# A hybrid encoder layer: the down projection as seven block products, and a first up tile evacuated product by product

## The chip, the cores and the metric

The kernel runs on one core of a Trainium2 chip. The metric is the device time of one execution in microseconds. Engines are named as in the profile: PE (TensorE), PEld (its weight loads), DVE (VectorE), ACT (ScalarE), POOL (GpSimd) and SP (SyncE, which issues nearly all transfers).

## The reference, cut to what matters

The layer is an attention mixer and a gated delta-rule mixer, then a feed-forward block with a causal convolution, then a per-layer embedding, and a last RMSNorm. Model width 1024, feed-forward width 2816, 1024 prompt frames and 8 x 16 sample frames, so T = 1152 columns. The change touches the feed-forward block alone:

```
h2 = _rmsnorm(x, norm_ffn)
u_gate, u_val = jnp.split(h2 @ w_up, [D_FF], axis=-1)
ext_f = jnp.concatenate([ffn_buf.astype(u_gate.dtype), u_gate], axis=1)
act = jax.nn.gelu(_causal_dwconv(ext_f, conv_ffn), approximate=True)
x = x + (act * u_val) @ w_down
gate_p = jax.nn.sigmoid(_rmsnorm(x, norm_ple) @ w_ple_gate)
x = x + gate_p * (p @ w_ple)
```

## The kernel before, in words

Everything is held transposed: features on the 128 partitions, frames along the columns. A float32 product is made of three fp32r matmuls: each operand is split into a rounded part H and a rest L, and the terms are wh x H, wh x L and wl x H. ACT makes H by a copy, DVE or POOL makes L by a subtraction.

**Who sets the order.** The program is recorded by coroutines. A driver (`_Driver`) keeps a planned clock for each engine and lets the thread go on that could start first; what it records is the fixed order of each engine's queue. `yield DVE` asks for an engine, `yield event` waits for another thread, `yield bank` takes a free buffer. `pick(DVE, POOL)` takes the engine whose planned clock is earlier.

**Up projection** (`up_products`, `evac_up`, `up_inner`). It has 22 tiles `ju[f]` of 128 + 128 features (gate and value). Each tile is seven half-size block products in the Strassen-Winograd manner, named A1X, S1T1, S2T2, A2X, S3T3, S4Y and B2T4; a product is 4 contraction tiles x 2 column halves x 3 terms = 24 matmuls of 288 columns. Three PSUM tiles `ups` serve them. The products in `CHAIN` are added onto an earlier product's PSUM tile, after that has been read (`kept`). The last read of a tile, of B2T4, multiplies by R2, the row factors of the RMSNorm. Sums of weight blocks (`up_sums`, tiles `s`) and weight splits (`up_rest`, tiles `wl`) are shared out by `pick`. `up_inner` does the convolution, the gelu and the product with the value half, and stores the 128 x 1152 result in DRAM as `AT[f]`.

**Down projection** (`jd`, `load_up`, `evac_down`). Three column blocks b of 384; in each two groups of four output row groups d; in each three pieces of the contraction (8, 8 and 6 tiles of 128). All weights are loaded and split again for every block, in three buffers (`down_weights`: wh/wl twice, T3H). The activations of a block are loaded from `AT` and split into the places that held the up projection's operands (B1, T0, T1, T2). `evac_down` multiplies by R2, adds the residual `x2T`, makes the operands H3/L3 of the gate and adds the squares to `ssq` (POOL).

**Gate blocks** (`gate`, `evac_pg`). Per block eight jobs of 24 matmuls of 384 columns on `w_ple_gate`; then a tanh, two multiply-adds on DVE and squares. The blocks 0 and 1 stand in the order after the first piece of the next column block's down products; block 2 is last. `final` scales and stores blocks 0 and 1, `last_rows` turns and stores block 2.

Two lines matter for the order of the row norms after the down projection: in `rms`, `if b < NB - 1: yield self.quarter[b + 1].done` holds block b's norm back until a job of the next block is through.

Of the kernel before, what the change touches and what calls it, by code (L numbers as in the profile page):

```python
# [297 lines left out]

def up_order(f):


    return (A1X, S1T1, A2X, S2T2, S4Y, S3T3, B2T4) if f == 0 else (A1X, S1T1, S2T2, A2X, S3T3, S4Y, B2T4)
# [6 lines left out]
class _Kernel:  # L309
# [95 lines left out]
    def down_loads(self):  # L405
# [6 lines left out]
        for j in self.jd:  # L412
# [35 lines left out]
    def down_weights(self, j, used):  # L448
# [14 lines left out]
        self.drv.spawn(self.down_rest(j, wh, wl), 1)  # L463
# [10 lines left out]
    def up_loads(self):  # L474

        nc = self.nc
        for j in self.ju:
# [8 lines left out]
            nc.sync.dma_start(g, self.I["w_up"][22 + j.f])  # L486
            nc.sync.dma_start(v, self.I["w_up"][j.f])
# [4 lines left out]
    def up_sums(self):  # L492
        nc, q = self.nc, {}
        for j in self.ju:
            yield j.loaded
            a1, a2, b1, b2 = j.raw
            for n in (0, 1, 3, 2) if j.f == 0 else range(4):
# [8 lines left out]
                e, w = self.pick(DVE, POOL) if j.f else (DVE, nc.vector)  # L506
                yield e
                (w.tensor_sub if n else w.tensor_add)(o, x, y)
# [3 lines left out]
    def up_weights(self, j, used):  # L512
# [8 lines left out]
        for i in up_order(j.f):  # L521
# [10 lines left out]
            self.drv.spawn(self.up_rest(j, i, wh, wl), 1 if j.f else 0)  # L532

    def up_rest(self, j, i, wh, wl):
        e, q = self.pick(DVE, POOL) if j.f else (DVE, self.nc.vector)
# [65 lines left out]
    def up_products(self, j):  # L601
        nc, drv = self.nc, self.drv
        bank = {}
        drv.spawn(self.evac_up(j, bank), 0 if j.f else -1)
        for i in up_order(j.f):
            yield j.prepared[i]
            wh, wl = j.w[i]
            if i in CHAIN:
                bank[i] = bank[CHAIN[i]]
                yield j.kept[CHAIN[i]]  # L610
            else:
                bank[i] = yield self.ups
            if (j.f, i) == (21, S3T3):
                drv.spawn(self.more_accs(), 1)
            first, own = i not in CHAIN, i in CHAIN
            for u in range(2):
                acc = bank[i][:, u, :288]
                for k in range(4):
# [4 lines left out]
                    nc.tensor.matmul(acc, wh[:, k], H, start=first and k == 0, stop=False, skip_group_check=own)  # L623
# [24 lines left out]
    def build(self):  # L648
# [28 lines left out]
        self.AT = dp.tile([22, 128, T], F32, name="AT")  # L677
        self.mixers()
        self.merge_ffn()

    def constants(self):
# [8 lines left out]
        t = cp.tile([128, 5], F32, name="ngd")  # L690
        self.ngd, self.ngf = t[:, 0:1], t[:, 1:5]
# [95 lines left out]
    def first_loads(self, jobs, p):  # L787
# [46 lines left out]
        nc.vector.tensor_scalar(self.ngf, self.nrm[:, 1, 0:4], -1.0, None, op0=OP.mult)  # L834
# [1596 lines left out]
    def merge_jobs(self):  # L2431
# [28 lines left out]
        self.aev = [[_Event() for _ in range(NB)] for _ in range(22)]  # L2460
        self.AB, self.H3, self.X4, self.jd, self.down = {}, {}, {}, [], []
        self.split3 = [_Event() for _ in range(4)]
        self.plev, self.aout = _Event(), [_Event() for _ in range(NB)]
        up = lambda k0: lambda k, cols: self.AB[k0 + k]

        self.piece, self.last = _Event(), None
# [3 lines left out]
        self.part_done, self.quarter = {}, {}  # L2470
# [7 lines left out]
        for b in range(NB):  # L2478
            for ds in (range(4), range(4, 8)):
                heads = {}  # L2480
                for k0, k1 in ((0, 8), (8, 16), (16, 22)):
                    if b and ds[0] == 0 and k0 == 8:

                        self.jd += gate(b - 1)
                    for d in ds:
                        j = _Job(I["w_down"][d][:, k0:k1], k1 - k0, up(k0), self.evac_down(d), blocks=(b,),
                                 pre=self.pre_down(d), late=True, head=heads.get(d), last=k1 == 22,
                                 need=lambda b, k, k0=k0: self.aev[k0 + k][b])
                        heads.setdefault(d, j)
                        self.jd.append(j)  # L2490
                        if k0 == 0 and d == 2:
                            self.quarter[b] = j
                        for f in range(k0, k1):
                            self.part_done[b, f] = j.done
        self.jd += gate(NB - 1)
        for j in self.ja+self.jo:
            j.merge = True
        a, b = self.jd[-8:-6]
        a.lag, a.twins, b.of = True, [b], a
        self.add_jobs(self.jpp + self.jb + self.ja + self.jo + self.ju + self.jd)  # L2500
# [121 lines left out]
    def evac_out(self, d):  # L2622
# [13 lines left out]
        def go(b, cols, acc, x):  # L2636
# [20 lines left out]
            if d < 4:  # L2657
# [5 lines left out]
                yield DVE  # L2663
                nc.vector.scalar_tensor_tensor(T1, lo, self.ngf[:, d:d + 1], T3, op0=OP.mult, op1=OP.add)
            else:
# [4 lines left out]
                yield from to(t, hi, T1, OP.subtract)  # L2670
# [29 lines left out]
    def up_parts(self, t):  # L2700
# [24 lines left out]
        if t == 3:  # L2725
            self.cs.views.append(self.hp.tile([128, 4, 2, 288], F32, name="T3")
                                 .rearrange("p a b c -> p (a b c)")[:, :T])
            self.cs.free.append((self.drv.cur.t, 0))

    def up_part(self, t, k, R, H, L, prev):  # L2730
# [4 lines left out]
        for b in range(NB):  # L2735
            self.drv.set(self.tev[t][k][b])

    def evac_up(self, j, bank):
# [8 lines left out]
        for i in up_order(f):  # L2747
# [3 lines left out]
            if i == S1T1 and f:  # L2751
                yield self.uev[f - 1]
            if i == B2T4:
# [7 lines left out]
                for e in self.Re[0]:  # L2761
                    yield e
                x = own(u3)
                q16 = lambda x: x.rearrange("p (b q) -> p b q", q=16)
                for o, i_, r in ((g[:, 1, :, :2], x[:, :, :2], R[:, 1, :, :2]),
                                 (ext[:, 962:1026], x[:, 0, 2, :64], self.R2[:, 960:TP]),
                                 (es[:, 0:2, 2:], q16(x[:, 0, 2, 64:]), q16(self.R2[:, TP:TP + 32])),
                                 (es[:, 2:8, 2:], q16(x[:, 1, 2]), q16(self.R2[:, TP + 32:]))):
                    yield DVE
                    nc.vector.tensor_mul(o, i_, r)  # L2770
# [551 lines left out]
```

## Time and profile before

| | |
|---|---|
| median of 3 runs | 2092.29 us (2091.4 to 2093.45) |
| the profiled execution | 2095.13 us, of which the span is 2093.4 us |
| granted clock, mean | 0.992 |
| PE busy | 2046.2 us, 98% of the span |
| DVE, ACT, POOL busy | 70%, 49%, 39% |
| up projection | 1190.9 to 1694.4 us |
| down projection and gate blocks | 1694.4 to 2082 us |
| last rows and output | 2082 to 2093.4 us |

A row of the windows view names a stretch in us from the span's start. `x` behind a busy time counts instructions. All work is recorded by helpers, so every line number is L192, and groups are told apart by their tiles: `up` and `dn` are the PSUM tiles of the two projections, `fe` the gate half with its convolution margin, `fv` the value half, `u` the partial sums of an up tile, `T` several tiles that take one another's place.

### The profile page before, as it was taken

How to read it: one execution, taken by the hardware profiler on the slowest of the kernel's cores; microseconds unless marked ns; L12 is line 12 of the kernel's file. 1: busy time of each engine (PE TensorE's matmuls, PEld its weight loads, DVE VectorE, ACT ScalarE, POOL GpSimd, SP SyncE). 2: the span in 40 equal slices, each digit the busy share in tenths (PEclk: the TensorE clock that was granted, in tenths of full speed). 3: DMA queues.
4: the chain of work that ended last, by engine and by line, in shares of the span. 5: the costliest groups of instructions: out<-in, count | busy, mean ns of one | idle time of the engine just before them, and what ended most of it. 6: DMA issues, size and time to landing. Idle time of an engine off the chain costs nothing.

```text
span 2093.4 us, 37189 instructions
## 1 busy us (share of the span) xinstructions
PE 2046.2 (98%) x13176; PEld 1997.7 (95%) x13176; DVE 1473.1 (70%) x3493; ACT 1034.4 (49%) x2057; POOL 816.3 (39%) x1025
## 2 busy tenths in 40 slices
PE   7999999999999999999999989999999999999998
PEld 6899999999999999989999989999999999999998
DVE  6268989998555687768465866666766675766656
ACT  5267667655634555676333433333333354535434
POOL 3344543532223534554363335555555500211102
PEclk9999999999999999999999999999999999999999
DMA  7343256776438564666664311212222266656542
GB/s 271 99 125 106 88 190 196 224 206 182 132 103 241 158 201 143 180 214 212 209 215 151 125 62 64 85 65 83 77 74 71 93 209 191 205 172 226 175 138 101
DMA packets 242697, 317.35 MB, mean 152 GB/s; under 512 B 40956, under 2 KB 200272, under 8 KB 242384
## 3 DMA queue, kind: packets, MB, share of 16 engines
q1 hardware_dynamic: 219712, 288.50, 44.6%
q10 hardware_dynamic: 22800, 26.49, 3.6%
q8 instruction: 104, 1.70, 0.3%
q14 instruction: 81, 0.66, 0.1%
HBM read 227.73 MB, written 88.81 MB: 151 GB/s over the span
## 4 chain that ended last, share of the span: by engine, by line
PE 53%; DVE 1%; DMA 1%; issue 0%; SPq 0%; ACT 0%; DVEq 0%; ACTq 0%
PE up L192 23%; PE dn L192 18%; PE acc L192 9%; PE at L192 1%; PE rp L192 0%; SPq L192 0%; DVE z L192 0%; DMA skr<-kTs 0%; DVE wl L192 0%; DMA skr<-in_ckT 0%; DMA evo<-gates 0%; DVE T L192 0%; DMA ppT<-evo 0%; DVE T0L L192 0%; DVE evo L192 0%
## 5 line engine op out<-in xcount | busy, mean ns | idle before, releaser
L192 PE MATMUL acc<-H,wh 128*128 128x384 f32 (+2 forms) x1344 | 474.6, 353 | 4.4 <-ACT evo L192 3.1
L192 PE MATMUL acc<-L,wh 128*128 128x384 f32 (+2 forms) x1344 | 455.8, 339 | 0.8 <-POOL L L192 0.5
L192 PE MATMUL acc<-H,wl 128*128 128x384 f32 (+2 forms) x1344 | 455.8, 339 | 0.4 <-POOL wl L192 0.4
L192 POOL TENSOR_TENSOR wl<-wr,wh 128x256 fp32r<-128x256 f32 (+1 forms) x267 | 228.6, 876 | 317.4 <-ACT wh L192 303.2
L192 PEld LDWEIGHTS acc<-H,wh 128*128 128x128 f32 (+1 forms) x1344 | 253.1, 188 | 12.8 <-ACT evo L192 3.8
L192 PEld LDWEIGHTS acc<-L,wh 128*128 128x128 f32 (+1 forms) x1344 | 253.1, 188 | 6.3 <-POOL L L192 1.9
L192 PEld LDWEIGHTS acc<-H,wl 128*128 128x128 f32 (+1 forms) x1344 | 252.5, 188 | 2.1 <-POOL wl L192 0.7
L192 POOL TENSOR_TENSOR ssq<-ssq,sqs 128x384 f32<-128x384 f32 x62 | 77.5, 1251 | 363.7 <-ACT sqs L192 356.9
L192 ACT CAST wh<-wr 128x1024 fp32r<-128x1024 f32 (+2 forms) x139 | 123.0, 885 | 142.5 <-PE up L192 40.7
L192 PE MATMUL up<-B,wh 128*128 128x288 f32 x704 | 143.5, 298 | 3.5 <-DVE fe L192 3.5
L192 DVE SCALAR_TENSOR_TENSOR T<-fe,cwf,T 128x512 f32<-128x512 f32 x132 | 107.5, 822 | 43.5 <-ACT T L192 41.2
L192 PEld LDWEIGHTS up<-B,wh 128*128 128x128 f32 x704 | 114.0, 190 | 3.7 <-DVE fe L192 3.7
L192 POOL TENSOR_TENSOR wl<-s,wh 128x256 fp32r<-128x256 f32 x86 | 71.6, 845 | 114.9 <-ACT wh L192 114.9
L192 ACT ACTIVATE ja<-SC,cola 128x768 bf16<-128x768 f32 (+2 forms) x93 | 96.8, 1041 | 25.0 <-DVE cola L192 17.5
L192 ACT COPY u<-up 128x576 f32<-128x576 f32 x66 | 42.3, 640 | 133.1 <-PE up L192 131.3
L192 PE MATMUL up<-B,wl 128*128 128x288 f32 x352 | 104.5, 297 | 0.0
L192 PE MATMUL up<-T,wh 128*128 128x288 f32 x352 | 104.0, 296 | 0.0
L192 ACT CAST wh<-s 128x512 fp32r<-128x512 f32 x88 | 52.4, 619 | 96.6 <-PE up L192 90.1
L192 DVE TENSOR_TENSOR wl<-wr,wh 128x512 fp32r<-128x512 f32 (+1 forms) x89 | 66.8, 765 | 31.9 <-ACT wh L192 31.9
L192 DVE TENSOR_SCALAR_CACHE_REDUCE e<-half,colv 128x384 bf16<-128x384 int16 (+5 forms) x96 | 71.2, 742 | 1.2
L192 POOL TENSOR_TENSOR cvc<-cvc,evo 128x384 f32<-128x384 f32 (+2 forms) x48 | 41.9, 876 | 73.6 <-ACT evo L192 50.6
L192 PEld LDWEIGHTS up<-T,wh 128*128 128x128 f32 x352 | 66.8, 190 | 0.0
(534 smaller groups left out, 6105.0 us busy)
## 6 DMA issues: line engine op xcount, KB each, us to landing
wr<-in_w_in SPq DMA_DIRECT2D x48, 512.0 KB, 3.6
AT<-fv SPq DMA_DIRECT2D x22, 576.0 KB, 2.8
wr<-in_w_down SPq DMA_DIRECT2D x24, 512.0 KB, 3.7
T<-in_w_down SPq DMA_DIRECT2D x24, 512.0 KB, 4.3
wr<-in_w_up SPq DMA_DIRECT2D x22, 512.0 KB, 3.5
gates<-evo ACTq DMA_DIRECT2D x48, 192.0 KB, 3.6
T<-AT SPq DMA_DIRECT2D x44, 192.0 KB, 4.2
qkv<-evo SPq DMA_DIRECT2D x36, 192.0 KB, 3.2
```

The source lines that it names most:

```text
L192: r = f(*a, **k)
```

## The change

1. **Down projection as seven block products** (`DN`, `down_all`). The output rows (2 x 512), the contraction (2 x 1408) and the columns (2 x 576) are halved. Product n needs for each of four row groups m a weight unit of 6 and one of 5 contraction tiles (`KU`), and the same 11 activations for all four m. A unit's matmuls run over two column halves of 288 for each contraction tile. There are no column blocks any more: the gate blocks 0, 1 and 2 follow the last product.
2. **Sums kept in DRAM.** The weight sums S1 to S4 are made during the up projection: `down_sums`, 16 steps, loads four pieces of `w_down`, does four additions or subtractions of at most 384 columns and stores four results, all through SP. The activation differences are made by `up_inner`: for f < 11 one subtraction before the store of `AT[f]`; for f > 10 it loads `AT[f-11]` again, makes three differences and stores `T4` and `T32`.
3. **Slots.** Activations go into 16 slots in B1, T0, T1 and T2, each loaded, split by ACT and DVE (`down_split`), and freed in the last of the four row groups.
4. **Evacuation** (`evac_down`). The results are added up in `X`; the rows of the first column half are complete after products 1 (A12 B21) and 4 (A22 T4), those of the second half after 5 and 6. Then come R2, the residual, the squares (`down_rows`) and the gate's operands (`down_norm`). The row norms wait for no later job.
5. **First up tile.** `evac_first` reads each of the seven products of tile 0 from a PSUM tile of its own and adds in SBUF. R2 is multiplied in afterwards, from SBUF (`gate_rest`).
6. **GpSimd.** `sooner` and `either` replace `pick` for the weight sums, splits and differences: DVE is taken unless POOL, at 2.3 times the cost, would end earlier by the planned clocks. The first two weight sums of a tile are always DVE's, in a form with the sign turned (so the signs of T1 and of a term in `evac_out` turn too).

```
+DN = "A11 B11", "A12 B21", "S2 T2", "S3 T3", "A22 T4", "S1 T1", "S4 B22"
+KU = (0, 6), (6, 11)
...
-                e, w = self.pick(DVE, POOL) if j.f else (DVE, nc.vector)
+                e, w = self.sooner(512) if j.f and n > 1 else (DVE, nc.vector)
...
-        drv.spawn(self.evac_up(j, bank), 0 if j.f else -1)
+        drv.spawn(self.evac_up(j, bank) if j.f else self.evac_first(j, bank), 0 if j.f else -1)
...
-            if i in CHAIN:
+            own = j.f > 0 and i in CHAIN
+            if own:
...
+        def add(i, o, x, last=True):
+            yield j.full[i]
+            y = bank[i][:, :, :288]
+            yield DVE
+            nc.vector.tensor_add(o, y if len(o.shape) == 3 else own(y), x)
+            if last:
+                drv.give(self.ups, bank[i])
...
+    def sooner(self, n):
+        d, c = self.drv, n * 1e-3
+        dve = max(d.clk[DVE], d.port[POOL]) + c
+        pool = max(d.clk[POOL], d.port[DVE]) + 2.3 * c
+        return (DVE, self.nc.vector) if dve <= pool else (POOL, self.nc.gpsimd)
...
+                yield from self.either("tensor_add", a22, a21, a22)
+                yield from self.either("tensor_sub", a21, a11, a21)
+                yield from self.either("tensor_sub", a11, a22, a11)
+                yield from self.either("tensor_sub", a12, a12, a11)
+                yield SP
+                for s, x in zip(("S1", "S3", "S2", "S4"), (a22, a21, a11, a12)):
+                    nc.sync.dma_start(self.SD[s][m][:, k0:k1], x.rearrange("p (k c) -> p k c", c=128))
...
+        for n in range(7):
+            for m in range(4):
+                bank = yield self.ups
...
+                    for k in range(k0, k1):
+                        yield self.dev2[n][k]
+                        H, L = self.dact[n, k]
+                        yield PE
+                        for u in range(2):
+                            acc, z = bank[:, u, :288], slice(u * 288, u * 288 + 288)
+                            nc.tensor.matmul(acc, wh[:, k - k0], H[:, z], start=k == 0, stop=False)
+                            nc.tensor.matmul(acc, wh[:, k - k0], L[:, z], start=False, stop=False)
+                            nc.tensor.matmul(acc, wl[:, k - k0], H[:, z], start=False, stop=k == 10)
+                        if m == 3:
+                            drv.give(self.slots, self.dact[n, k])
...
     def rms(self, b, cols, ev):
-        if b < NB - 1:
-            yield self.quarter[b + 1].done
```

What the planner makes of it stands in the engines' orders. The first place is DVE at the end of up tile 0, where the row factors R come into use (`fe` is the gate half, `u` a partial sum, `wl` and `s` weights of the next tile). Before:

```order
L192 TENSOR_TENSOR s_14717<-wr,wr_14537 128x512
L192 TENSOR_TENSOR fe_14601<-u_14363,R_12795 128x2x2x96
L192 TENSOR_TENSOR fe_14601<-u_14363,R_12795 128x64
L192 TENSOR_TENSOR wl<-wv,wh 128x512
L192 TENSOR_TENSOR fe_14601<-u_14363,R_12795 128x2x16
L192 TENSOR_TENSOR fe_14601<-u_14363,R_12795 128x6x16
L192 TENSOR_TENSOR fe_14601<-up_13383,R_12795 128x2x3x96
```

And now:

```order
L192 TENSOR_TENSOR s_14717<-wr,wr_14542 128x512
L192 TENSOR_TENSOR xs_14681<-xs_14680,xs_14681 128x384
L192 TENSOR_TENSOR xs_14680<-xs_14678,xs_14680 128x384
L192 TENSOR_TENSOR xs_14678<-xs_14681,xs_14678 128x384
L192 TENSOR_TENSOR xs_14679<-xs_14679,xs_14678 128x384
L192 TENSOR_TENSOR fe_14417<-fe_14417,R_12800 128x2x3x96
L192 TENSOR_TENSOR fe_14417<-u_14365,R_12800 128x2x2x96
```

The multiplication that read the PSUM tile `up` reads SBUF now, and the first weight sums (`xs`) stand ahead of it.

The second place is the middle of the up projection. POOL before, where `s` are sums of up weights and `wl` the rest of a split, by halves:

```order
L192 TENSOR_TENSOR s_16160<-wr,wr_15999 128x512
L192 TENSOR_TENSOR wl<-s_15971,wh 128x256 x2
L192 TENSOR_TENSOR s_16216<-wr,s_16102 128x512
L192 COPY cfs<-fe_16059 128x18
L192 TENSOR_TENSOR wl<-wr,wh 128x256 x2
L192 TENSOR_TENSOR s_16294<-wv 128x512
L192 MEMSET fe_16303 128x2
```

DVE now, between two additions into `fv` (`T<-fv,T` is a difference of activations):

```order
L192 TENSOR_TENSOR s_18580<-wg,s_18478 128x512
L192 SCALAR_TENSOR_TENSOR T_14605<-fe_18433,cwf,T_14605 128x128
L192 TENSOR_TENSOR xs_18498<-xs_18496,xs_18498 128x256
L192 TENSOR_TENSOR xs_18496<-xs_18499,xs_18496 128x256
L192 TENSOR_TENSOR xs_18497<-xs_18497,xs_18496 128x256
L192 TENSOR_TENSOR fv_18585<-up_14361,u_18455 128x2x3x96
L192 TENSOR_TENSOR fv_18326<-fv_18326,T_14605 128x576 x2
L192 TENSOR_TENSOR wl<-wg,wh 128x512
L192 TENSOR_TENSOR u_18457<-up_14360,u_18457 128x576
L192 TENSOR_TENSOR T_14605<-fv_18326,T_14605 128x576
L192 TENSOR_TENSOR fv_18585<-up_13386,u_18456 128x2x3x96
```

The sum `s` has come over from POOL, the `xs` rows and `T<-fv,T` are new; they stand in one queue with the reads of `up` that PE's later products need.

The third place is DVE in a gate block (`dn` is the gate's PSUM tile). The last block before:

```order
L192 TENSOR_TENSOR gt_22014<-dn_19720,R_12795 128x384
L192 TENSOR_TENSOR wl<-T_19688,wh 128x512
L192 SCALAR_TENSOR_TENSOR gt_22014<-gt_22014,pp_21977 128x384
L192 TENSOR_TENSOR wl<-T_19688,wh 128x512
L192 SCALAR_TENSOR_TENSOR B_19646<-gt_22014,B_19646 128x384
L192 TENSOR_TENSOR gt_22055<-dn_19719,R_12795 128x384
```

The second block now (`L<-B,nrm,H` makes the third block's operands, `rr` and `rs` are a row norm):

```order
L192 TENSOR_SCALAR rr_m<-rp_23002 128x3
L192 SCALAR_TENSOR_TENSOR L_22939<-B_19943,nrm,H_22938 128x384
L192 TENSOR_SCALAR rs_i<-rr_m 128x3
L192 TENSOR_SCALAR rr_r<-rs_i 128x3
L192 TENSOR_TENSOR gt_23033<-dn_22565,R_12800 128x384
L192 TENSOR_TENSOR rs_a<-rr_r 128x3
```

The operands of a later block and a row norm stand between the reads of `dn`.

More of the change, by code (lines that the diff above doesn't have):

```diff
@@ L622, in up_products @@
                     yield PE
-                    nc.tensor.matmul(acc, wh[:, k], H, start=first and k == 0, stop=False, skip_group_check=own)
+                    nc.tensor.matmul(acc, wh[:, k], H, start=k == 0 and not own, stop=False, skip_group_check=own)
                     nc.tensor.matmul(acc, wh[:, k], L, start=False, stop=False, skip_group_check=own)
@@ L2477, in gate @@
             return [job(d) for d in range(8)]
[L2478 to L2495, printed above, removed]
+        self.jd = gate(0) + gate(1) + gate(2)
+        self.ju_last = self.du[-1].done
         for j in self.ja+self.jo:
             j.merge = True
-        a, b = self.jd[-8:-6]
-        a.lag, a.twins, b.of = True, [b], a
-        self.add_jobs(self.jpp + self.jb + self.ja + self.jo + self.ju + self.jd)
+        self.add_jobs(self.jpp + self.jb + self.ja + self.jo + self.ju + self.du + self.jd)
     def merge_loads(self, prev, last):
@@ L2760, in evac_up @@
                 nc.gpsimd.tensor_copy(es[:, :, 0:2], self.scf[:, f])
[L2761 to L2770, printed above, removed]
+                yield from self.gate_rest(g, ext, es, own(u3))
                 drv.set(self.uev[f])
@@ L2854, in evac_down @@
[L2854 to L2870 removed]
+            nc.scalar.copy(u2(U), y)
@@ new lines, in squares, with down_norm @@
+    def squares(self, x, d, cols, first):
+        nc, drv = self.nc, self.drv
+        ssq = self.ssq[:, cols]
+        yield ACT
+        if first:
+            nc.scalar.activation(ssq, x, AF.Square)
+            return
+        s = yield self.sqs
+        s_ = s[:, :cols.stop - cols.start]
+        yield ACT
+        nc.scalar.activation(s_, x, AF.Square)
+        yield POOL
+        nc.gpsimd.tensor_add(ssq, ssq, s_)
+        drv.give(self.sqs, s)
+    def down_norm(self, b):
+        nc, drv = self.nc, self.drv
+        cols = slice(b * BW, b * BW + BW)
+        pool, names = (self.hp, ("B1", "T1")) if b == 1 else (self.wp2, ("H3", "L3"))
+        if b:
+            yield self.ju_last if b == 1 else self.jd[8 * b - 9].done
+        self.H3[b] = [pool.tile([128, KD, BW], F32R, name=n, bufs=1) for n in names]
+        H, L = self.H3[b]
+        for d in range(8):
+            for h in ((0,), (0, 1), (1,))[b]:
+                yield self.xev4[d][h]
+            y, g = self.X[:, d, cols], self.nrm[:, 2, d:d + 1]
@@ L3043, in last_rows @@
         yield self.allt
+        if self.turned3 is None:
+            self.turned3 = self.hp.tile([128, 3072], F32, name="B1")
+        out = self.turned3
         r = self.rlast[z]
```

343 lines of the change are left out of this document (249 added, 94 removed).

## The prediction

> **What bounds the kernel now.** I read the windows by stage first, then what TensorE waited for, then single instructions. The columns of a window are its stretch and length, then busy time and count of PE, PEld, DVE, ACT and POOL, the granted clock, the DMA share and GB/s.
>
> ```profile
> PE 2046.2 (98%) x13176; PEld 1997.7 (95%) x13176; DVE 1473.1 (70%) x3493; ACT 1034.4 (49%) x2057; POOL 816.3 (39%) x1025
> 1190.90:1240.00 49.10, 43.03 (x302) 42.30 (x301) 33.97 (x55) 21.63 (x39) 19.34 (x18) 0.93 0.23 73
> 1240.00:1500.00 260.00, 260.00 (x1963) 260.00 (x1962) 176.14 (x231) 98.97 (x163) 147.51 (x168) 1.00 0.21 73
> 1694.40:1818.00 123.60, 123.60 (x714) 123.60 (x713) 81.89 (x150) 60.20 (x90) 11.80 (x9) 1.00 0.67 215
> 2048.00:2082.00 34.00, 33.42 (x217) 33.33 (x216) 24.10 (x57) 18.43 (x34) 10.03 (x7) 1.00 0.21 67
> 2082.00:2093.40 11.40, 4.35 (x25) 4.11 (x25) 3.93 (x20) 1.85 (x4) 0.00 (x0) 0.65 0.36 138
> ```
>
> From 1240 to about 2080 us PE runs without a gap, through the up projection (until 1694.4) and the down projection with its gate blocks. PE sets the end: matmul time taken out there is time gained, for as long as the other engines keep up. Only two stretches are not full: the first 49 us of the up projection (6.1 us idle) and the last 11.4 us. What PE waited for in the up projection, in us, times, longest:
>
> ```profile
> PE up L192 <- DVE fe L192: 3.5, 1, 3.5
> PE up L192 <- DVE u L192: 2.2, 1, 2.2
> PE up L192 <- DVE T0L L192: 0.3, 1, 0.3
> ```
>
> Each is one single wait, and all three belong to up tile 0 and the step to tile 1.
>
> **The matmuls.** The down projection now has 3 column blocks x 8 row groups x 22 contraction tiles x 3 split terms = 1584 matmuls of 384 columns. The change makes it 7 products x 4 row groups x 11 contraction tiles x 2 column halves x 3 terms = 1848 of 288 columns. The clean stretch at 288 columns is 1240 to 1500 above; these two are clean at 384:
>
> ```profile
> 1700.00:1798.00 98.00, 98.00 (x562) 98.00 (x561) 64.40 (x109) 47.46 (x70) 11.11 (x7) 1.00 0.67 212
> 1855.00:1925.00 70.00, 70.00 (x402) 70.00 (x401) 46.66 (x78) 34.65 (x53) 10.69 (x7) 1.00 0.66 208
> ```
>
> 260.00/1963 = 132.5 ns for 288 columns, 98.00/562 = 174.4 ns for 384 (70.00/402 = 174.1). Per column 0.460 against 0.454 ns: the narrow form loses little. Removed 1584 x 174.4 = 276.2 us, added 1848 x 132.5 = 244.9 us: **-31.3 us**. The 576 gate matmuls and the small row-norm matmuls stay.
>
> **Up tile 0.** Its 168 matmuls stay, but each product gets a PSUM tile of its own and is read out without the row factor R. That removes what the two longer waits were for:
>
> ```profile
> 1213.76 0.74 DVE L192 TENSOR_TENSOR u<-up,u 128x576 f32<-128x576 f32 x1
> 1230.79 0.48 ACT L192 COPY R<-rp 128x384 f32<-128x384 f32 x1 [1.38 <-PE rp L192]
> 1233.85 0.75 DVE L192 TENSOR_TENSOR fe<-up,R 128x576 f32<-128x576 f32 x1
> ```
>
> The 2.2 us were the last product, chained onto the tile that DVE was still reading (first row); without a chain it can start at once. The 3.5 us were tile 1 waiting for a PSUM tile that was only read once R had come (the other two rows). Bounds: -5.7 us if both go, 0 if they come back elsewhere. They could: DVE has seven PSUM reads here instead of four (3 x 0.75 = 2.3 us more, against two copies fewer on ACT), and R's multiplies now follow four weight-sum instructions on DVE that wait for a load. Queued behind them is the release of a buffer that tile 1's third product is copied into, and PE's fifth product of tile 1 waits for that. One product's time, 3.2 us, lies between. I take **-5 us**.
>
> **The other 21 up tiles.** Here the change adds work on DVE and takes it from POOL. Two windows of one tile's length (168 x 132.5 ns = 22.3 us), then groups of instructions with their mean ns (the one of 346 from the stage behind, where POOL does little):
>
> ```profile
> 1400.00:1422.30 22.30, 22.30 (x170) 22.30 (x169) 13.90 (x18) 8.97 (x15) 12.48 (x14) 1.00 0.21 74
> 1600.00:1622.30 22.30, 22.30 (x170) 22.30 (x169) 16.55 (x23) 8.28 (x14) 13.35 (x16) 1.00 0.21 67
> L192 DVE TENSOR_TENSOR wl<-s,wh 128x512 fp32r<-128x512 f32 x40 | 39.5, 988 | 15.4 <-ACT wh L192 15.4
> L192 DVE TENSOR_TENSOR s<-s,wg 128x512 f32<-128x512 f32 x9 | 10.9, 1207 | 18.5 <-POOL wl L192 18.5
> L192 DVE TENSOR_TENSOR wl<-wr,wh 128x512 fp32r<-128x512 f32 x11 | 7.5, 681 | 0.0
> L192 DVE TENSOR_TENSOR fv<-fv,T 128x576 f32<-128x576 f32 x42 | 40.9, 1008 | 6.5 <-ACT T L192 6.5
> L192 DVE SCALAR_TENSOR_TENSOR T<-fe,cwf,T 128x512 f32<-128x512 f32 x81 | 67.4, 843 | 32.6 <-ACT T L192 30.7
> L192 DVE SCALAR_TENSOR_TENSOR T<-fe,cwf,T 128x128 f32<-128x128 f32 x42 | 34.4, 818 | 10.1 <-ACT T L192 9.7
> L192 DVE SCALAR_TENSOR_TENSOR T<-fe,cwf,T 128x128 f32<-128x128 f32 x2 | 0.7, 346 | 0.0
> L192 DVE TENSOR_TENSOR T0L<-xs,T0H 128x384 fp32r<-128x384 f32 x3 | 1.6, 546 | 0.0
> L192 POOL TENSOR_TENSOR wl<-s,wh 128x256 fp32r<-128x256 f32 x80 | 66.9, 848 | 105.3 <-ACT wh L192 105.3
> ```
>
> In the order of the program DVE gets, per tile, 4.9 more instructions of 512 columns that were POOL's, 2.9 weight sums of at most 384, and 2.1 differences of 576. POOL is left with 3.3 of 256 and some small copies: about 3.9 us instead of 12 to 13. The same 512-column subtraction took DVE 681 ns undisturbed and 988 to 1207 beside POOL, so I bound the additions. Undisturbed: 4.9 x 0.68 + 2.9 x 0.55 + 2.1 x 0.75 = 6.5 us. At the disturbed rows: 4.9 x 1.1 + 2.9 x 0.85 (0.55 raised alike) + 2.1 x 1.0 = 10.0 us. On 15.2 (the mean of the two windows) that is 21.7 to 25.2 us of 22.3. But the 15.2 hold at least 3.1 us of disturbance themselves (3.2 x 0.3 for wl, 2.1 x 0.25 for fv, 4 x 0.16 and 2 x 0.47 for the convolution), and with two thirds of POOL's work gone I take two thirds of that off: 21.7 - 2.1 = **19.6 us of 22.3**, 88%. DVE keeps up, with less reserve than now. On the loads' side SP gets 143 more issues over the program; the up weights queued behind the stores of the new sums are fetched a tile ahead (22 us), and a load takes 3.5 to 4.2 us (rows in the next part). Inside a tile PE waits for DVE's add on the fifth product, for which there is one product's time, 3.2 us. For late adds I put **+2 us** over the whole stage, between 0 and the case of rival D.
>
> **Down products.** One contraction tile is 6 x 132.5 = 0.80 us of PE. Sixteen slots hold eleven activations and five of the next product; an entry's slot is freed 11.9 us before PE wants the new entry (8.75 us for one row group, plus four tiles). It needs a load, a copy and a subtraction:
>
> ```profile
> T<-AT SPq DMA_DIRECT2D x44, 192.0 KB, 4.2
> wr<-in_w_up SPq DMA_DIRECT2D x22, 512.0 KB, 3.5
> wr<-in_w_down SPq DMA_DIRECT2D x24, 512.0 KB, 3.7
> 1193.73 1.25 ACT L192 CAST T0H<-T 128x576 fp32r<-128x576 f32 x2
> 1193.61 0.75 DVE L192 TENSOR_TENSOR T0L<-T,T0H 128x576 fp32r<-128x576 f32 x1
> 1194.28 0.35 DVE L192 TENSOR_TENSOR T1L<-sqs,T1H 128x192 fp32r<-128x192 f32 x1
> ```
>
> 4.2 + 0.6 + 0.75 = 5.6 us, so 6 us in reserve. DVE's share over the seven products is 77 x 0.75 for splits, 28 x 1.9 for weights (1408 columns at 0.68 per 512), 28 x 0.75 for evacuation, 32 x 0.75 for R and the residual: 156 us of 245, 64%, about as in the stretch from 1694 now. I cost the evacuations at nothing: three PSUM tiles give each 17.5 us. If that cover went, each would cost PE its own 1 to 3 us, 28 times.
>
> **Gate blocks.** They stood in the midst of the down projection, with the final scaling of a block under the next block's products. Now all three follow each other, and the norms of blocks 1 and 2 and two final scalings fall into them:
>
> ```profile
> L192 DVE TENSOR_TENSOR gt<-dn,R 128x384 f32<-128x384 f32 x47 | 25.9, 554 | 33.9 <-PE dn L192 32.4 <-issue 1.4
> L192 DVE SCALAR_TENSOR_TENSOR gt<-gt,pp 128x384 f32<-128x384 f32 x23 | 13.3, 576 | 0.7 <-ACT gt L192 0.6
> L192 DVE SCALAR_TENSOR_TENSOR B<-gt,B 128x384 f32<-128x384 f32 x23 | 12.6, 552 | 0.1
> L192 DVE TENSOR_TENSOR wl<-T,wh 128x512 fp32r<-128x512 f32 x56 | 40.8, 746 | 31.2 <-ACT wh L192 30.6 <-DMA T<-in_w_ple_gate 0.6
> L192 DVE SCALAR_TENSOR_TENSOR L<-B,nrm,H 128x384 fp32r<-128x384 f32 x24 | 14.7, 612 | 0.9 <-ACT H L192 0.4
> L192 DVE SCALAR_TENSOR_TENSOR B<-B,nrm,rp 128x384 f32<-128x384 f32 x10 | 5.4, 608 | 0.9 <-ACT gt L192 0.9
> L192 DVE SCALAR_TENSOR_TENSOR rs_a<-rs_a,rr_m 128x3 f32<-128x3 f32 x15 | 2.4, 161 | 0.4
> L192 DVE TENSOR_TENSOR T3H<-T,T3H 128x512 fp32r<-128x512 f32 x3 | 3.7, 1235 | 2.1 <-ACT T3H L192 2.1
> 1820.00:1830.00 10.00, 10.00 (x59) 10.00 (x58) 6.45 (x12) 5.03 (x8) 2.06 (x3) 1.00 0.49 149
> ```
>
> Per block DVE has 8 x (0.554 + 0.576 + 0.552) + 16 x 0.746 + 8 x 0.612 = 30.3 us, and in the second 5 x 0.608 and a row norm of 11 x 0.161 = 1.8: 35.2 us of durations. Consecutive ones overlap a little, about a tenth by my estimate (the instruction of 0.75 us at 1193.61 above is followed by the next after 0.67), so some 32 us against 192 x 174.4 = 33.5 us and two row-norm groups of PE. That is close to full. Six PSUM tiles let DVE lag by 20 us before PE stops for evacuation, but weights are only two jobs ahead. **+1.5 us**; the ends are 0 and rival B. The last gate job and the output are the same instructions in the same order as now, so the tail stays at 13.4 us.
>
> **Sum.** -31.3 - 5 + 2 + 1.5 = -32.8. The profiled execution took 2095.1 us for a span of 2093.4, so I expect a span near 2060.6; the median of the runs shown, 2092.3, becomes **2059.5 us**.
>
> **Rivals.** A is the forecast, 2054 to 2066.
>
> B: DVE becomes the bound of the gate blocks. For it: 32 of 34 us, and the row of 1235 ns in the last block. Then a block has 16 x (1.235 - 0.746) = 7.8 us more, 40 against 34.7, over two blocks about +10: 2070. Against it: in the first gate block now (the window above) DVE has 6.45 us in 10 and never holds PE.
>
> C: the supply of the down products is late. SP issues in order, and at the step from up to down the slot and weight loads stand behind stores that wait for tiles 20 and 21. With two weight loads ahead (3.7 each) and a load half as long again (6.3), 13.7 + 1.4 us against 11.9 makes 3.2 us, six times: +19, 2079.
>
> D, the other side: DVE does not keep up in the up tiles. At the disturbed rows 25.2 us a tile against 22.3 is 21 x 2.9 = +61, so 2059.5 - 2 + 61 = 2118. It decides from 24.0 us a tile (22.3 + 34.8/21). Against it: POOL's share falls to a third.
>
> E: a narrow matmul costs as much as a wide one, 264 x 174.4 = +46.0 in place of -31.3: about 2137. The up rows at 132.5 ns speak against it. The Trainium skill, TensorE: Matmul & The Clock Gate, section Back-to-back issue gap, points that way: it gives about 81 ns at 128 columns and 131 at 512 for a sustained stream, from which I estimate 102 at 288 and 114 at 384, and the down projection would get 7 us dearer. By that rule the change would not pay; this trace does not agree (132.5 and 174.4 ns).
>
> **How the numbers follow.** A 0.75, B 0.10, C 0.07, D 0.05, E 0.02, and 0.01 for no difference. A measurement of this kernel can tell about 0.2%, 4.2 us. Faster: A, B, C = 0.92; within: 0.01, and 0.01 of D's weak form; slower: 0.06. The range must hold 8 in 10: A with its ends and B's, **2053 to 2075**.
>
> **What would show it.** PE's windows at 132 to 133 ns a matmul through all seven products; no wait of PE on `fe` and at most 1 us on `u` in tile 0; a DVE share near 88% in an up tile with waits of PE on `u` or `wl` of 2 us at most; DVE over 90% in the second gate block. The prediction is wrong if PE waits for DVE in most up tiles (D), for `H` or `wh` at each change of product (C), or if down matmuls lie at more than 136 ns.

## The result, and the profile after

| | before | after |
|---|---|---|
| median | 2091.88 us (2091.4 to 2093.45) | 2056.95 us (2053.47 to 2058.31) |
| the profiled execution | 2095.13 us, span 2093.4 | 2056.07 us, span 2053.9 |
| first up matmul | 1190.9 us | 1189.1 us |
| up projection | 503.5 us | 494.7 us |
| down projection and gate blocks | 385.3 us | 358.0 us |
| from the last gate matmul to the end | 13.6 us | 12.2 us |

The ratio is 0.9829, with a 95% interval of 0.9812 to 0.9846: 35 us less. The forecast was 2059.5, in a range of 2053 to 2075. The stages come from the first and last matmuls of each in the two traces; their differences are -1.9, -8.9, -27.3 and -1.4 us, together the 39.4 us between the two spans. (The profiled run of the kernel before lay 3 us above its median, hence 39 and not 35.)

The line of busy times on the page of the changed kernel:

```profile
PE 2012.5 (98%) x13440; PEld 1964.8 (96%) x13440; DVE 1531.5 (75%) x3702; ACT 1024.1 (50%) x2062; POOL 659.5 (32%) x879
```

Its windows over the stages (as before: PE, PEld, DVE, ACT, POOL busy with their counts, then granted clock, DMA share and GB/s):

```profile
1194.90:1223.30 28.40, 28.28 (x214) 28.00 (x215) 25.70 (x50) 11.40 (x21) 8.85 (x5) 1.00 0.25 83
1223.30:1500.00 276.70, 276.70 (x2088) 276.70 (x2088) 220.16 (x380) 106.38 (x178) 52.79 (x80) 1.00 0.45 144
1500.00:1685.90 185.90, 185.90 (x1404) 185.90 (x1403) 151.87 (x253) 78.32 (x131) 35.98 (x56) 1.00 0.54 186
1686.00:1760.00 74.00, 74.00 (x560) 74.00 (x559) 51.08 (x88) 35.01 (x57) 7.77 (x7) 1.00 0.73 240
1760.00:1930.60 170.60, 170.60 (x1289) 170.60 (x1289) 107.92 (x179) 68.76 (x112) 33.97 (x29) 1.00 0.54 176
1930.60:1968.00 37.40, 37.40 (x226) 37.40 (x225) 33.68 (x73) 22.89 (x38) 10.23 (x9) 1.00 0.52 168
1968.00:2003.00 35.00, 34.85 (x203) 34.53 (x202) 30.58 (x59) 20.81 (x36) 11.17 (x9) 1.00 0.49 157
2003.00:2007.90 4.90, 2.98 (x18) 2.66 (x16) 4.90 (x9) 1.44 (x4) 1.59 (x2) 1.00 0.83 255
2009.80:2013.20 3.40, 3.40 (x13) 3.40 (x12) 3.26 (x10) 1.23 (x3) 0.00 (x0) 0.50 0.83 303
```

The seven down products (1686 to 1930.6) are full at 132.1 and 132.3 ns a matmul. The first hole behind the row-norm products is at 2005.5 to 2007.9, in the first job of the third gate block, and at 2009.8 begins a stretch at half clock. What PE waited for from the first up matmul to the end:

```profile
PE dn L192 <- DVE L L192: 1.9, 1, 1.9
PE rp L192 <- ACT sqs L192: 0.7, 1, 0.7
PE up L192 <- DVE T0L L192: 0.3, 1, 0.3
```

Both waits of the up projection before (3.5 on `fe`, 2.2 on `u`) are gone. There is one new wait, on an `L` of the gate. Two questions came out of this: why the up stage gained 8.9 us when the two waits were 5.7, and why the gate blocks gave 4 us back.

For the first, windows of the kernel before, right behind its two stalls:

```profile
1214.60:1220.00 5.40, 5.35 (x29) 5.38 (x30) 4.88 (x10) 0.00 (x0) 4.16 (x2) 0.68 0.00 0
1234.60:1240.00 5.40, 5.35 (x29) 5.35 (x30) 2.51 (x4) 2.16 (x4) 0.61 (x2) 0.68 0.22 89
```

The granted clock is 0.68 there: 3.41 us of the 5.4 at half speed, in which the 288-column matmuls come every 240 instead of 132.6 ns. That is about 14 x 107 ns = 1.5 us a stall, which the prediction didn't count. 5.7 + 2 x 1.5 = 8.7, close to the 8.9 measured. My theory at this point: tile 0's singles (part 5: each product read from a PSUM tile of its own) took away both stalls and both slow stretches. The rivals: the stalls alone count, or the gain came from the new share of work between DVE and POOL.

### The profile page after: what moved, and what is told of

Read it like the earlier page. It is cut to its first block, busy times and chain, and to the rows that moved or that the text cites. A ratio compares the mean times of both kernels' runs of the same rounds, so it can differ in the third digit from the quotient of the medians.

```text
span 2053.9 us, 37994 instructions
## 1 busy us (share of the span) xinstructions
PE 2012.5 (98%) x13440; PEld 1964.8 (96%) x13440; DVE 1531.5 (75%) x3702; ACT 1024.1 (50%) x2062; POOL 659.5 (32%) x879
## 4 chain that ended last, share of the span: by engine, by line
PE 86%; DVE 5%; DMA 3%; ACT 1%; issue 1%; POOL 1%; SPq 0%; ACTq 0%; DVEq 0%; POOLq 0%
PE up L192 36%; PE acc L192 34%; PE at L192 7%; PE dn L192 4%; PE gd L192 3%; PE ix L192 1%; DMA obT<-sg 1%; DVE z L192 1%; PE rp L192 0%; SPq L192 0%; DVE e L192 0%; DMA ppT<-evo 0%; DMA sg<-sgb 0%; DVE cvc L192 0%; DMA kL<-kTs 0%
## 5 line engine op out<-in xcount | busy, mean ns | idle before, releaser
L192 PE MATMUL up<-B,wh 128*128 128x288 f32 x1272 | 257.1, 296 | 0.0
L192 PE MATMUL up<-T,wh 128*128 128x288 f32 x1012 | 243.4, 295 | 0.0
L192 PEld LDWEIGHTS up<-B,wh 128*128 128x128 f32 x1272 | 204.1, 188 | 0.0
L192 PEld LDWEIGHTS up<-T,wh 128*128 128x128 f32 x1012 | 174.1, 188 | 0.1
L192 ACT CAST wh<-wr 128x1024 fp32r<-128x1024 f32 (+3 forms) x134 | 114.2, 852 | 114.8 <-PE acc L192 42.1
L192 PEld LDWEIGHTS up<-B,wl 128*128 128x128 f32 x636 | 119.4, 188 | 0.0
L192 PE MATMUL up<-T0L,wh 128*128 128x288 f32 x296 | 87.4, 295 | 0.3 <-DVE T0L L192 0.3
L192 PE MATMUL up<-T0H,wh 128*128 128x288 f32 x296 | 87.4, 295 | 0.0
L192 PE MATMUL up<-T0H,wl 128*128 128x288 f32 x296 | 87.1, 294 | 0.0
L192 PE MATMUL up<-T,wl 128*128 128x288 f32 x294 | 87.1, 296 | 0.0
```

What stands on the lines that cost most here:

```text
L192: r = f(*a, **k)
```

## Experiments

A gap, below, is the time from one weight load of PE to the next; a matmul of 288 columns makes a regular one of 0.13 us.

### Tile 0's singles alone, and all but the singles

The kernel before with the new evacuation of tile 0 and nothing else (`evac_first` and the exchanged order of tile 0's weights are cut here and below):

```
-        drv.spawn(self.evac_up(j, bank), 0 if j.f else -1)
+        drv.spawn(self.evac_up(j, bank) if j.f else self.evac_first(j, bank), 0 if j.f else -1)
...
-            if i in CHAIN:
+            own = j.f > 0 and i in CHAIN
+            if own:
```

> The kernel before, with one part of the change alone: up tile 0 has all eight PSUM groups evacuated singly; the down projection stays as it was. Theory (a stall costs its own time and the half-clock window of 3.4 us that follows it): in the kernel before the two gaps of 2.6 and 3.9 us around up tile 0 were each followed by a window of 3.4 us in which about 14 of the 288-column products came every 240 instead of 132.6 ns, 1.5 us each. With the singles both gaps and both windows go: about -8.7 us against the kernel before, a ratio of 0.9958. Rival 1 (only the gaps count, the clock would have stepped down there anyway): -5.7 us, 0.9973, with the windows still at the start of the up stage. Rival 2 (VectorE, which takes the evacuations, is late in tile 1 in place of tile 0): about 0.

And the changed kernel with tile 0 the old way:

```
-        drv.spawn(self.evac_up(j, bank) if j.f else self.evac_first(j, bank), 0 if j.f else -1)
+        drv.spawn(self.evac_up(j, bank), 0 if j.f else -1)
...
-            own = j.f > 0 and i in CHAIN
+            own = i in CHAIN
```

> The changed kernel, with up tile 0 evacuated in the old way (chained in pairs through R). Theory (stall plus half-clock window): +8.7 us against the changed kernel, a ratio to the kernel before of about 0.987, with two gaps of 2 to 4 us and two windows at half clock near the ends of tile 0. Rival 1 (gaps alone): +5.7 us, 0.9857. Rival 2 (the rest of the -8.85 us seen between the two traces comes from the new share of work between VectorE and GpSimd): +3 us or less.

The theory missed both times. The singles alone: 2090.93 us against 2093.08, a ratio of 0.9995 (0.9983 to 1.0007; the two medians alone would give 0.9990). In the trace the up stage is 4.1 us shorter, which is a little more than the interval of the times allows; it is far from 8.7 in either. The changed kernel without the singles: 2058.89 us, 0.9843 (0.9829 to 0.9856), only some 2 us above the changed kernel, and not 8.7; this is what rival 2, the new share, had said. PE's longest wait at the start of the up stage in the first of the two:

```profile
PE up L192 <- ACT u L192: 3.2, 1, 3.2
```

What ACT did there (start, us, and in brackets what it had waited for):

```profile
1231.92 0.48 ACT L192 COPY R<-rp 128x384 f32<-128x384 f32 x1 [0.59 <-PE rp L192]
1233.82 0.72 ACT L192 ACTIVATE T<-fe,cwf 128x512 f32<-128x512 f32 x1 [1.42 <-DVE fe L192]
1234.44 0.62 ACT L192 COPY u<-up 128x576 f32<-128x576 f32 x1
```

The first stall is gone, the second has stayed and only changed its name. Now ACT holds PE: the copy of tile 1's PSUM tile (`u<-up`) stands behind a convolution step of tile 0 (`T<-fe,cwf`), which waits for `fe`, which waits for R. So the chain begins with R, and R is late because its three products stand late on PE. In the traces they come after 219, 228 and 237 up matmuls in the kernel before and after 252, 261 and 264 in this one; in the changed kernel after 204, 213 and 222. (The next two expectations give lower counts; those here are of all up matmuls ahead in the trace.) There the last copy of R begins 34.3 us after the first up matmul, in place of 39.6 in this run:

```profile
1223.33 0.48 ACT L192 COPY R<-rp 128x384 f32<-128x384 f32 x1 [0.82 <-PE rp L192]
```

So the singles alone did not free the second wait. But this run moved R's products later as well, by 27 to 33 up matmuls (some 4 us); what the singles do with R in its old place, no run shows. What moved R's products forward had to be in part 6 of the change, and a new theory said so in numbers.

R's place was not the whole of the wait in the kernel before. There the last copy of R ended at 1231.3 and PE went on at 1234.65. In between DVE had this row ahead of the last multiplications by R:

```profile
1232.33 0.80 DVE L192 TENSOR_TENSOR wl<-wv,wh 128x512 fp32r<-128x512 f32 x1 [0.81 <-ACT wh L192]
```

That is 1.6 us of the 3.5 (0.81 idle and 0.80 busy) for a weight split that merely stood in the queue. In the kernel with the new rules alone, below, it no longer stands there, and R comes earlier too; no run parts the two.

### GpSimd's rules alone, and with the singles

```
-                e, w = self.pick(DVE, POOL) if j.f else (DVE, nc.vector)
+                e, w = self.sooner(512) if j.f and n > 1 else (DVE, nc.vector)
...
-            self.drv.spawn(self.up_rest(j, i, wh, wl), 1 if j.f else 0)
+            self.drv.spawn(self.up_rest(j, i, wh, wl), 0)
...
-        e, q = self.pick(DVE, POOL) if j.f else (DVE, self.nc.vector)
+        e, q = self.sooner(512) if j.f else (DVE, self.nc.vector)
```

> The kernel before, with the rules for GpSimd alone (the share by where the operation would end first, the first two weight sums of a tile on VectorE, weight splits at priority 0, the convolution's steps in the new order); down projection and tile 0 as before. In the run with tile 0's singles alone the gap of 3.6 us at the start of tile 1 stayed, with the three products that make the row factors R standing 232 to 240 products into the up stage (203 to 221 in the kernel before, 164 to 180 in the changed kernel). Theory now (the second stall belongs to R's place, which the new share sets, and the singles remove the first alone): here R's products stand after 176, 191 and 200 up products, the second gap (3.9 us) and the half-clock window behind it go, the first gap of 2.6 us shrinks to some 1.4: about -6.5 us in the up stage, 0.997. Rival (the second stall went with the singles and the new share together, each alone does nothing for it): -1 us or less, the gap of over 3 us still there.

With the singles added:

> The kernel before, with the singles of tile 0 and the rules for GpSimd together, and the old down projection: all of the change but its main part. Theory (singles for the first stall, R's place for the second): both gaps and both half-clock windows go, -8.5 us in the up stage against the kernel before, 0.996; the rest of the gain, about 27 us, belongs to the down projection. Rival: R's products stand at 188 to 206 here (164 to 180 in the changed kernel), late enough that a stall stays in tile 1: -4 us.

The rules alone: 2085.45 us, 0.9966 (0.9955 to 0.9978), and 8.0 us less in the up stage. The second stall and its slow stretch are gone, and of the first a gap of 1.4 us is left, with no slow stretch behind it. R's products come after 192, 207 and 216 up matmuls. (The convolution's new order, which was in this kernel too, leaves them at 219, 228 and 237 in the planner's order when it is put in by itself; the rule for the weight sums by itself puts them at 195, 207 and 216. Neither kernel was run.) PE's wait there:

```profile
PE up L192 <- DVE u L192: 1.0, 1, 1.0
```

With the singles as well, that goes too: 2085.31 us, 0.997 (0.9958 to 0.9982), up stage 494.5 us, 9.0 less than before and the same as in the changed kernel (494.7). So the rules for GpSimd, with the convolution's new order, are worth 8.0 of the 9 us in the up stage; the singles add 1.0 behind it, or 4.1 without it. In the times, which vary by some us with the mixers ahead, the two are alike. (The rival's premise doesn't hold: in the traces R's products come after 204, 213 and 222 up matmuls in this kernel and in the changed one.)

This pair settles two more points. The changed kernel is the second of them with the new down projection: 2056.95 against 2085.31, so the block products are worth 28 us. And it makes the weight sums and activation differences during the up stage, which this kernel doesn't have. Windows of the kernel with the rules and the singles:

```profile
1223.30:1500.00 276.70, 276.70 (x2088) 276.70 (x2088) 186.87 (x318) 108.30 (x179) 52.06 (x85) 1.00 0.23 76
1500.00:1683.60 183.60, 183.60 (x1387) 183.60 (x1386) 123.02 (x212) 73.74 (x126) 34.36 (x58) 1.00 0.25 82
```

In the first of them DVE is busy for 186.9 us in place of 220.2 in the changed kernel, the DMA engines 23% in place of 45%, and PE does the same 2088 matmuls in both. The 33 us of sums and differences and the doubled traffic cost the up stage nothing.

### GpSimd's share by the earlier clock again

```
     def sooner(self, n):
-        d, c = self.drv, n * 1e-3
-        dve = max(d.clk[DVE], d.port[POOL]) + c
-        pool = max(d.clk[POOL], d.port[DVE]) + 2.3 * c
-        return (DVE, self.nc.vector) if dve <= pool else (POOL, self.nc.gpsimd)
+        return self.pick(DVE, POOL)
```

> The changed kernel, with the share of work between VectorE and GpSimd decided again by the earlier planned end of an engine's queue instead of by where the operation itself would end first; GpSimd takes 906 instead of 705 of the rows that may go to either. Theory: in the up stage VectorE has slack (80% busy), so the share decides nothing there so long as no tile of GpSimd's comes late; GpSimd's operations take two to three times VectorE's and slow VectorE's beside them: 0 to +4 us, where the plus comes from waits for evacuations that GpSimd holds. Rival 1 (relief of VectorE in the gate blocks is what counts): -2 to -4 us, the gap at 2007.9 us gone. Rival 2 (the up tiles of the changed kernel need the new share): +40 us or more, with PE waits in each up tile.

2072.28 us, 0.9904 (0.989 to 0.9919): 15 us above the changed kernel, between the theory and rival 2. PE's largest wait of that kernel:

```profile
PE up L192 <- DVE u L192: 10.3, 3, 5.4
```

Its convolution step among the groups of DVE in the up stage, and under it the same step in the changed kernel (count, busy us, mean ns):

```profile
L192 DVE SCALAR_TENSOR_TENSOR T<-fe,cwf,T 128x512 f32<-128x512 f32 x81 | 90.5, 1133 | 0.8 <-ACT T L192 0.8
```

```profile
L192 DVE SCALAR_TENSOR_TENSOR T<-fe,cwf,T 128x512 f32<-128x512 f32 x84 | 61.9, 750 | 7.2 <-ACT T L192 7.2
```

The up stage is 15.9 us longer than in the changed kernel (510.5 against 494.7). The step takes 1133 instead of 750 ns when POOL does more beside it. Ahead of the longest wait (gap 5.8 us, ending at 1531.8) four of these steps in a row took 4.3 us, while POOL worked without a pause:

```profile
1520.43 4.32 DVE L192 SCALAR_TENSOR_TENSOR T<-fe,cwf,T 128x512 f32<-128x512 f32 x4
1527.54 1.10 DVE L192 TENSOR_TENSOR wl<-s,wh 128x512 fp32r<-128x512 f32 x1 [2.79 <-ACT wh L192]
1528.57 1.08 DVE L192 SCALAR_TENSOR_TENSOR T<-fe,cwf,T 128x128 f32<-128x128 f32 x1
1530.91 0.74 DVE L192 TENSOR_TENSOR u<-up,u 128x576 f32<-128x576 f32 x1
1523.02 1.18 POOL L192 TENSOR_TENSOR wl<-wr,wh 128x256 fp32r<-128x256 f32 x1
1524.16 1.19 POOL L192 TENSOR_TENSOR wl<-wg,wh 128x256 fp32r<-128x256 f32 x1
```

DVE's slowness is only part of it: in the second row DVE had stood idle for 2.8 us until ACT had a `wh` (the bracket), and ACT for 5.2 us before that, for a reason that the profile doesn't name. The three gaps make 11 us, and two stretches at half clock follow, of 6.8 and 3.4 us. So with the sums of the down projection in the up stage the choice by where an operation would end is what keeps PE from waiting there. It is not what brings R early: in this run R's products come after 201, 213 and 222 up matmuls, as in the changed kernel. That must be one of the rules that this run keeps, such as the first two weight sums always on DVE. How much of the three waits is DVE's slowness beside POOL and how much is the order of the queues, this run doesn't part.

### The late L in the gate blocks

```
-                drv.spawn(self.down_norm(b), 2)
+                drv.spawn(self.down_norm(b), 0)
```

(The number is the planner's priority; 2 comes last.) The third gate block begins at 2001.8, and its first job needs the eighth and last L of its operands at 2005.5; PE's gap there is 2.4 us. The L are made during the second block, in which the expectations place the stall. Rows of ACT and DVE in the changed kernel: ACT has the eighth H at 1986.5, and DVE makes the L that belongs to it 20 us later, behind other work.

```profile
1985.93 0.60 ACT L192 ACTIVATE H<-B,nrm 128x384 fp32r<-128x384 f32 x1
2006.72 0.60 DVE L192 SCALAR_TENSOR_TENSOR B<-B,nrm,rp 128x384 f32<-128x384 f32 x1
2007.25 0.60 DVE L192 SCALAR_TENSOR_TENSOR L<-B,nrm,H 128x384 fp32r<-128x384 f32 x1
```

> The changed kernel, with the planner's priority of the operation that makes L (B times norm plus H) set to 0 in place of 2, so that in the second gate block it stands on VectorE ahead of evacuations that are not yet due. Theory: the gap of 2.4 us that PE has at 2007.9 us on the last L of that block goes, and with it the half-clock window behind it (11 products at 320 instead of 174.5 ns, 1.6 us): about -3.9 us against the changed kernel, some 2053 us, 0.9811 of the kernel before. Rival (VectorE is full there, and whatever is made earlier makes an evacuation late): the gap comes back as a wait for a PSUM bank or on another operand in the same block, 0 to -1 us.

2052.08 us, 0.9812 (0.9798 to 0.9825). In a second comparison the changed kernel itself ran in the same rounds:

> The changed kernel as it is, on the same chip and in the same rounds as the next one: 2057 us, 0.983 of the kernel before.

> The changed kernel with the operation that makes L at priority 0, once more beside the changed kernel itself. Theory (the one late L cost its stall of 2.3 us and 1.6 us of half clock): 3 to 4.5 us under the changed kernel, about 0.981 of the kernel before. Rival (the 4.9 us between the two medians came from the mixers, whose half-clock windows lie elsewhere in each run): within 1 us of it.

2056.18 us for the changed kernel (0.982, 0.9806 to 0.9834), 2053.47 for this one (0.9809, 0.9796 to 0.9823). The medians are 4.9 and 2.7 us apart, and the intervals overlap. The traces are clearer, since they can leave the mixers out: from the first to the last gate matmul 107.5 and 107.4 us with the L early, 111.2 and 112.8 without. PE waits for nothing in the gate blocks of the version with the early L; this is all it waits for after the mixers (second run):

```profile
PE up L192 <- DVE T0L L192: 0.3, 1, 0.3
```

The last L for the third block is done at 1986.3 there, during the second:

```profile
1985.19 1.08 DVE L192 SCALAR_TENSOR_TENSOR L<-B,nrm,H 128x384 fp32r<-128x384 f32 x1
```

And the window of the second block:

```profile
1971.00:2007.00 36.00, 35.89 (x209) 35.32 (x208) 31.85 (x62) 21.71 (x36) 10.65 (x9) 1.00 0.53 175
```

DVE has as much to do in that block as in the changed kernel (31.85 of 36 us, 88%; 87% there), and no evacuation came late instead. It was an order, not a bound. By the traces and by the medians this is the fastest version found; one digit makes it.

### What a stall costs

```
+STALL = {(1, 1): 1, (1, 3): 5, (2, 1): 2, (2, 3): 6, (3, 1): 3, (3, 3): 7, (4, 1): 4, (4, 3): 8, (5, 1): 6, (5, 3): 5}
...
+                    if c == 0 and (n, m) in STALL:
+                        yield ACT
+                        nc.scalar.copy(self.ngd, self.prev[:, 1, :1])
+                        for _ in range(STALL[n, m]):
+                            yield ACT
+                            nc.scalar.copy(wh[:, :2], wh[:, :2].bitcast(F32))
                     for k in range(k0, k1):
```

(The copies were 1 to 8, not 2 to 10 as the expectation says.)

> The changed kernel, with ten stalls of PE put into the down products, at least 17 us apart: ahead of a unit ScalarE reads a value of the last unit's PSUM tile and then copies a piece of the weights' high half onto itself 2 to 10 times, and the next product waits for that. Lengths by the copies (about 0.4 us each): some 1.2, 1.6, 2.0, 2.4, 2.4, 2.8, 2.8, 3.2, 3.6 and 4.4 us. Theory (an idle time of about 2.1 us or more inside one stretch of the 3.4 us grid is followed by 3.4 us of half clock, in which 288-column products come every 240 ns): the stalls under 2 us cost their own time, those over 2.4 us 1.5 us more, so 28 us of stalls and six or seven times 1.5 us, in all +37 us against the changed kernel. Rival (the clock steps down only after a whole idle stretch of 3.4 us, or at times of its own): +28 to 31 us, windows behind at most the two longest.

2101.29 us, 44.3 above the changed kernel. The stalls came out longer than planned: 34.6 us in all (the gaps below less the regular 0.13 us each). The rest is 9.7 us, about what some 90 matmuls at 240 ns in place of 132.5 make (90 x 107). Gaps and the clock that follows, from the starts of weight loads and the clock's records:

```
gap, us   then, at half clock
1.76      -
2.21      -
2.64      -
3.07      3.4 us
3.51      3.4 us
3.95      -
4.23      3.4 us
4.38      3.4 us
4.39      6.8 us
5.82      6.8 us
```

Windows of 3 us behind the stalls of 2.64 and 4.38 us:

```profile
1810.60:1813.60 3.00, 3.00 (x23) 3.00 (x24) 0.00 (x0) 0.00 (x0) 0.00 (x0) 1.00 0.46 131
1833.30:1836.30 3.00, 3.00 (x15) 3.00 (x14) 0.00 (x0) 0.21 (x1) 0.00 (x0) 0.50 0.54 144
```

23 matmuls in the one, 15 in the other. The theory is right in kind: a stall has a second price. My threshold was too sharp. Over all runs, of 6 single gaps of 1.4 to 2.2 us none was followed by half clock, of 8 gaps of 2.4 to 2.7 us five were, and of 11 gaps over 3 us ten. The same gap of 2.43 us in the gate blocks was followed by 3.4 us in one run of the changed kernel, by 6.8 in another, and by none in the run with fewer slots below. It matters how the gap lies on the clock's grid: the stretches start at multiples of 3.413 us from one another in a trace (before: 1214.7 and 1235.2, six steps), so that the idle time of a gap falls into one step of this grid or into two. Over all traces, from the first up matmul to the last gate matmul, each of the 14 steps with 2.2 us or more of idle time was followed by one at half clock, and none of those with less than 1.1; of 29 steps in between 8 were. So a bound of about 2 us is right for most steps and not for all.

The Trainium skill, TensorE: Matmul & The Clock Gate, section Part 1: The HAM clock gate, has the window of 4096 cycles or 3413 ns and says that it runs freely; the traces agree. Its section on HAM oscillation asks for no idle gaps over about 3.4 us; these traces show half clock after gaps from 2.4 us on.

### Fewer slots

```
+NSLOT = 11
...
             for z in range(0, 2304, HW):
+                if n >= NSLOT:
+                    break
```

> The changed kernel with 11 in place of 16 activation slots, so that the activations of a product are loaded only when those of the product before are freed, one by one, in the last row group of four. Theory (a load, the split on ScalarE and VectorE take about 6 us, and the next product's first activation is needed 11 x 0.8 us = 8.7 us after its slot is freed): no wait, 0 to +2 us against the changed kernel. Rival (supply of activations bounds the down products as soon as the reserve is short): a wait of some 3 us ahead of each of the six products after the first, +18 us and more with half-clock windows.

2067.78 us, 0.9884 (0.9871 to 0.9898): 11 us above the changed kernel, between the two. PE's waits in the down products, then pieces of the chain of waits that ends in the longest of them:

```profile
PE up L192 <- DVE T L192: 4.3, 6, 1.8
PE up L192 <- DVE T0L L192: 2.2, 5, 0.5
```

```profile
1754.29 7.07 DMA T<-T
...
1761.38 0.67 ACT T L192
1762.05 0.64 ACT wh L192
...
1763.32 0.75 DVE T L192
1764.07 0.60 DVE wl L192
1764.67 0.68 DVE T L192
```

From the issue of the load until PE may go on (1765.4) it takes 11.1 us: 7.1 for the load, 4 for the splits, which stand in turn with those of the weights. That is twice the 5.6 us I had summed. The waits shown make 6.5 us; with the shorter gaps around them and 1.8 us at half clock behind two gaps in a row (1.7 and 1.1 us) the down products take 258.7 in place of 246.5 us. With 11 slots PE waits; with 16, where an entry has 4 us more, it never does. The prediction's 11.9 us for an entry was enough, but its reserve, if its worst entry is as slow as this one, is about 1 us (11.9 - 11.1) and not 6. The trace of the changed kernel agrees: of the activations of products 2 to 7 the tightest is the tenth of the third product, whose split ended on DVE at 1759.4 and which PE first used at 1761.0, 1.6 us later.

## Why the prediction was right, point by point

**Matmuls, -31.3 us.** Right: 132.1 to 132.3 ns a matmul through the down products, no wait, and 246.6 us for the stage against 244.9 forecast for its 1848 matmuls. Rival E and the rule quoted with it fall with that row.

**Tile 0, -5 us; measured -8.9 for the whole up stage.** The size was off, and so was one reason. The step that failed is "That removes what the two longer waits were for". The singles did this for the wait on `u`. The wait on `fe` began with R, and a wait of 3.2 us stayed with the singles alone; it went where the rules for GpSimd moved R's products forward on PE and a weight split out of DVE's way. So both waits went as forecast, but the second for another reason than the one given: that part of the term was right by luck. The part that was missing in the price is the half clock behind each stall, 1.5 us each.

**The other up tiles, +2 us.** Mis-sized; nothing was lost: the kernel with the rules and singles but without sums has the same up stage (494.5 and 494.7). DVE's share is 80 to 82% (220.16 of 276.7, 151.87 of 185.9), where I had forecast 88%. What was underrated is how much of DVE's busy time was slowness beside POOL. The kernel before had 231 DVE instructions and 176.1 us busy in 260 us; with the rules and the singles it is 318 and 186.9 in 276.7, which is 299 and 175.6 in 260. DVE took over 68 instructions at no busy time at all. Two groups in that kernel, which took 988 and 1008 ns each in the prediction's rows:

```profile
L192 DVE TENSOR_TENSOR wl<-s,wh 128x512 fp32r<-128x512 f32 x59 | 45.8, 777 | 54.4 <-ACT wh L192 54.4
L192 DVE TENSOR_TENSOR fv<-fv,T 128x576 f32<-128x576 f32 x38 | 28.7, 778 | 0.0
```

(The steps of the convolution became faster as well, but their order changed too, so they don't tell.) Rival D (25.2 us a tile) was further away than the 5% it got; with the old share beside the new sums, 15 us of loss showed what it would have been like.

**Down products, 0.** Right in the number, wrong in the reserve: 1.6 us where 6 had been summed. By the run with 11 slots rival C was nearer than I had thought.

**Gate blocks, +1.5 us; measured +4.0** (27.3 gained in place of 31.3). The term was mis-sized, and rival B named the wrong mechanism. DVE was busy for 87% of the second block, where the forecast was over 90%, and for 90% of the first, but fullness was not what stopped PE. One instruction for the third block stood 20 us late in DVE's order: 2.3 us of stall and 1.6 of half clock. Placed earlier, it cost nothing.

**Tail, 0; measured -1.4.** It was 13.3 to 13.8 us in the runs with the old down projection and 11.4 to 12.7 in those of the changed kernel and of the early L. I made no run for the cause; it is open.

**The sum.** The forecast of the span, 2060.6, was 6.7 us above the trace: 5.9 in the up stage and 1.4 in the tail on the one side, 2.5 in the gate blocks on the other, and 1.9 that lie in the mixers ahead, which the change doesn't touch (the first up matmul lies between 1187.4 and 1193.5 in the runs of this study). The time hit as well as it did because the errors partly cancelled.

## What to carry to other kernels

Price a PE stall by what follows it as well: where it exceeds about 2.4 us, look at the granted clock behind it before you say what removing it is worth. When a wait ends on an engine, follow it to the operand that came last (here R) and look at what orders that operand; the engine named by the wait may change while the stall stays. On an engine that is 90% busy in a fixed order, a low priority can hold an instruction until its consumer stands still, so check the deadlines of such instructions before you call the engine the bound.

## What I had not expected of the hardware

- The half clock after a stall: 3.41 us long, sometimes 6.8, in which a 288-column matmul comes every 240 ns instead of 132.5 and a 384-column one every 320 instead of 174.5. Ten stalls of 34.6 us cost 44.3 us.
- Taking two thirds of POOL's busy time over to DVE left DVE's busy time where it was (176.1 us in 260, and 186.9 in 276.7, which is 175.6 in 260).
